# Moving the output projection's evacuation, root steps and row scaling off VectorE in a hybrid RG-LRU / stick-breaking-attention block

## The chip, the cores and the metric

The kernel runs as one program on one core of a Trainium2 chip. The metric is the device time of one execution in microseconds (us), as the median of several. The engines of the core are called here as the profile calls them: PE (TensorE, matrix products), DVE (VectorE), ACT (ScalarE), POOL (GpSimd) and SP (the queue from which all transfers of this kernel start). Each engine works through its own list of instructions in order. An instruction that waits for another engine holds up everything behind it on its own engine.

## The reference

One block of a language model on 2048 rows of width 1024, in float32:

```python
h  = rms_norm(x, norm_mix);  u = h @ w_in
lru_x, lru_g, q, k, v = split(u, [512] * 5)
y_lru = gelu(lru_g) * rg_lru(conv4(lru_x))            # linear recurrence over the rows
y_att = stick_breaking_attention(q, k, v)             # 8 heads of 64, causal
y  = concat(rms_norm(y_lru), rms_norm(y_att))
x  = x + y @ w_out                                    # the output projection
h2 = rms_norm(x, norm_ffn);  gu = h2 @ w_ffn_in
x  = x + (silu(gu[:2816]) * gu[2816:]) @ w_ffn_out
out = rms_norm(x, norm_final)
```

Stick-breaking attention has, for each query, `beta = sigmoid(z)` per key and a running product of `sigmoid(-z)` from the newest key to the oldest. The weight of a key is its beta times the product over the newer keys.

## The kernel before

Every float32 product is made of three products of split operands (`mm3`, L147 to L151: a high part rounded to fp32r, and a low part, the rest). The 2048 rows are four groups of 512 (`g`). The program has three stages: the mixer (up to some 1245 us), the first feed-forward product, and the second with the final norm. The change is in the mixer alone.

In the mixer the attention of group g is the main line (`attention`, `drive`), cut into items of 128 queries by up to 512 keys of one head. `drive` puts one iteration per item on the list and, between its steps, pieces of other work (the "fill"). Iteration i holds four steps of four different items:

- `score` of item i+4: PE forms `z`, ACT makes the two sigmoids `u` and `be` (L362, L363), POOL sets the last column of `u` to one (L360) and, in diagonal blocks, masks `u` and `be` (L366);
- `scan` of item i+2: the running product over `u` on DVE (L372);
- `weights` of item i+1: `be` times `u` on DVE (L378);
- `turn` of item i: PE transposes `be` into the PSUM tile `t`, ACT copies the high part `ah` out (L394), DVE takes the low part `al` (L395). Two iterations later `weigh` multiplies by the values (L408).

`u` has four buffers, `z` and `t` two each. For the first three groups the fill is the input projection of the next group. For the last group (from 805 us on) it is the output projection of all four groups, `mix_out`. It runs through eight jobs (g, br), br 0 for the recurrent half of y and br 1 for the attention half. A job (`Mix.run`) has eight PSUM tiles `po` of 128 rows by 512 columns, each the sum of 24 matmuls; after each, one DVE instruction (L671) multiplies the tile by the row's norm factor `rs` and adds it to the rows `x2` (named `xo` in the trace). After the second tile of a job `following.take` loads the four tiles `yt` of the next job, splits them (`yhi` on ACT, `ylo` on DVE L638), squares them on ACT and sums the squares on POOL (`acc`, L646). After the seventh tile `sums` has PE sum the squares over the channels (`pss`), and `rsqrt_mean` works out `rs` on tiles of 128x4: four DVE steps and three rounds of Newton's method with three DVE instructions each (L133, L135, L137).

After br 1 `store_rows` stores the rows and squares them on ACT (eight `sqf`, L695), and a second `rsqrt_mean` gives their factor `rsf` for the next norm. For the groups 0 and 1 `turn_rows` then scales the four row tiles, two on DVE (L707) and two on ACT (L705), waits `REST` = 8 pieces of fill during which only attention is on PE's list, and lets PE transpose the rows (`h2t`, L713). The last job, (3, 1), runs after the attention has ended.

PE's list is in the order in which the code is written (`manual_schedule`). The lists of DVE, ACT, POOL and SP are put in order by a scheduler that goes by its own estimates of durations and by priorities; the attention's steps have a higher priority than the fill. Small tiles of the fill (`yt`, `sqf`, the transposed rows `h`) share one pool, `stg` with tag `s`, of four buffers used in turn.

Of the kernel before, what the change touches and what calls it, by code (L numbers as in the profile page):

```python
# [9 lines left out]
F32 = mybir.dt.float32  # L10
F32R = mybir.dt.float32r
I32 = mybir.dt.int32
AF = mybir.ActivationFunctionType
ALU = mybir.AluOpType
# [3 lines left out]
P = 128  # L18
S = 2048
D = 1024  # L20
KD = D // P
LRU = 512
# [5 lines left out]
GT = 512  # L28
HT = 1024
NG = S // GT  # L30
TPG = GT // P
# [59 lines left out]
def tile_block(ctx: ExitStack, tc: tile.TileContext, x, w_in, w_out, w_gu, w_dn,  # L91
               g_mix, g_ffn, g_y, g_fin, lru_p, w_gate, out):
    nc = tc.nc
# [24 lines left out]

    smp = ctx.enter_context(tc.tile_pool(name="smp", bufs=2))

    def rsqrt_mean(ss, n, width, name):

        v = smp.tile([P, n], F32, tag=f"v{n}", name=f"{name}_v")
        nc.vector.tensor_scalar(out=v, in0=ss, scalar1=1.0 / width, scalar2=EPS, op0=ALU.mult, op1=ALU.add)  # L124
        t = smp.tile([P, n], I32, tag=f"t{n}", name=f"{name}_t")
        nc.vector.tensor_single_scalar(t, v.bitcast(I32), 1, op=ALU.arith_shift_right)
        y = smp.tile([P, n], F32, tag=f"y{n}", name=f"{name}_y", bufs=3)
        nc.vector.tensor_scalar(out=y.bitcast(I32), in0=t, scalar1=-1.0, scalar2=float(0x5F3759DF),
                                op0=ALU.mult, op1=ALU.add)
        nc.vector.tensor_scalar(out=v, in0=v, scalar1=-0.5, scalar2=None, op0=ALU.mult)  # L130
        for it in range(3):
            a = smp.tile([P, n], F32, tag=f"a{n}", name=f"{name}_a{it}")
            nc.vector.tensor_tensor(out=a, in0=y, in1=y, op=ALU.mult)  # L133
            b = smp.tile([P, n], F32, tag=f"b{n}", name=f"{name}_b{it}")
            nc.vector.tensor_tensor(out=b, in0=a, in1=v, op=ALU.mult)  # L135
            y2 = smp.tile([P, n], F32, tag=f"y{n}", name=f"{name}_y{it}", bufs=3)
            nc.vector.scalar_tensor_tensor(out=y2, in0=b, scalar=1.5, in1=y, op0=ALU.add, op1=ALU.mult)  # L137
            y = y2
        return y

# [2 lines left out]
    rsf = const.tile([P, S // P], F32, name="rsf")  # L143
# [14 lines left out]
    stg = base.enter_context(tc.tile_pool(name="stg", bufs=4, side="left"))  # L158
# [403 lines left out]
    def prep(g):  # L562
# [45 lines left out]
        for c in range(WC // P - 1):  # L608
            yield from proj_col(g, cg, c, w, keep_qk(g))
            if g == NG - 1:  # L610
                first[0].sums()

        turns = make_ht(g + 1, xs) if xs else iter(())
        for k, _ in enumerate(proj_col(g, cg, WC // P - 1, w, keep_qk(g))):
# [8 lines left out]
    class Mix:  # L623
# [21 lines left out]
                nc.scalar.activation(sq, yt, AF.Square)  # L645
                nc.gpsimd.tensor_tensor(out=self.acc, in0=self.acc, in1=sq, op=ALU.add)  # L646

        def sums(self):
            pss = ps_d.tile([P, GT], F32, tag="d", name=f"pss{self.nm}")
            for t in range(TPG):  # L650
                nc.tensor.matmul(pss[:, t:t + 1], lhsT=self.acc[:, t * P:(t + 1) * P], rhs=ones,
                                 start=True, stop=True)
            ss = smp.tile([P, TPG], F32, tag="ssy", name=f"ssm{self.nm}")
            nc.vector.tensor_copy(ss, pss[:, :TPG])
            self.rs = rsqrt_mean(ss, TPG, LRU, f"ry{self.nm}")

        def run(self, x2, following=None, ready=NCT):
            for n in range(D // GT):
                halves = [next_half(), next_half()]
                ns = slice(n * GT, (n + 1) * GT)  # L660
                for t in range(TPG):
                    ts = slice(t * P, (t + 1) * P)
                    po = ps_d.tile([P, GT], F32, tag="d", name=f"po{self.nm}_{n}_{t}")
                    for i, (hi, lo) in enumerate(halves):
                        for c in range(NCT):
                            yh, yl = self.split[c]
                            mm3(po[:, i * WC:(i + 1) * WC], yh[:, ts], yl[:, ts], hi[:, c], lo[:, c],
                                c == 0, c == NCT - 1)
                            if c == 1 or (c == NCT - 1 and i == 0):
                                yield  # L670
                    nc.vector.scalar_tensor_tensor(out=x2[t][:, ns], in0=po, scalar=self.rs[:, t:t + 1],  # L671
                                                   in1=x2[t][:, ns], op0=ALU.mult, op1=ALU.add)
                    yield
                    if following and (n, t) == (0, TPG // 2 - 1):
                        for c in range(ready):
                            following.take(c)
                    if following and ready == NCT and (n, t) == (1, SUMS):
                        following.sums()

    def load_rows(g):  # L680
        x2 = []
# [6 lines left out]
    def store_rows(g, x2):  # L688

        ss = smp.tile([P, TPG, 2], F32, tag="ssx", name=f"ssf{g}")  # L690
# [4 lines left out]
                nc.scalar.activation(sq, x2[t][:, i * 512:(i + 1) * 512], AF.Square, accum_out=ss[:, t, i:i + 1])  # L695
        s2 = smp.tile([P, TPG], F32, tag="ssy", name=f"ssg{g}")
        nc.vector.tensor_tensor(out=s2, in0=ss[:, :, 0], in1=ss[:, :, 1], op=ALU.add)
        nc.vector.tensor_copy(rsf[:, g * TPG:(g + 1) * TPG], rsqrt_mean(s2, TPG, D, f"rf{g}"))

    def turn_rows(g, x2):  # L700

        for t in range(TPG):
            r = rsf[:, g * TPG + t:g * TPG + t + 1]
            if t % 2:
                nc.scalar.activation(x2[t], x2[t], AF.Copy, scale=r)  # L705
            else:
                nc.vector.tensor_scalar(out=x2[t], in0=x2[t], scalar1=r, scalar2=None, op0=ALU.mult)  # L707
        for _ in range(REST):
            yield
        for k in range(KD):  # L710
# [558 lines left out]
```

## Time and profile before

| | |
|---|---|
| time, median of 3 runs | 2646.09 us (2645.66 to 2648.19) |
| profiled execution | 2647.3 us, its span 2645.6 us |
| PE busy, whole span | 2430.8 us (92%), mean granted clock 0.969 |
| DVE busy, whole span | 1842.4 us (70%) |
| ACT busy, whole span | 1262.6 us (48%) |
| POOL busy, whole span | 1204.0 us (46%) |

Busy shares are means over stages with different limits, so the rows of the section below are taken from the stage in question, 805 to 1195 us. A row that groups instructions gives line, engine, operation, tiles out and in, shapes and count, then busy time and mean duration of one, then the engine's idle time just before them and what ended it. In a timeline two instructions of one engine overlap a little: the next one starts some 0.08 us before the one ahead is recorded as ended.

### The profile page before, as it was taken

How to read it: one execution, taken by the hardware profiler on the slowest of the kernel's cores; microseconds unless marked ns; L12 is line 12 of the kernel's file. 1: busy time of each engine (PE TensorE's matmuls, PEld its weight loads, DVE VectorE, ACT ScalarE, POOL GpSimd, SP SyncE). 2: the span in 40 equal slices, each digit the busy share in tenths (PEclk: the TensorE clock that was granted, in tenths of full speed). 3: DMA queues.
4: the chain of work that ended last, by engine and by line, in shares of the span. 5: the costliest groups of instructions: out<-in, count | busy, mean ns of one | idle time of the engine just before them, and what ended most of it. 6: DMA issues, size and time to landing. Idle time of an engine off the chain costs nothing. (4 is left out here: it accounts for less than half of the span.)

```text
span 2645.6 us, 36918 instructions
## 1 busy us (share of the span) xinstructions
PE 2430.8 (92%) x12680; PEld 2046.7 (77%) x12680; DVE 1842.4 (70%) x2575; ACT 1262.6 (48%) x2285; POOL 1204.0 (46%) x1420
## 2 busy tenths in 40 slices
PE   7999999999888797897899979989999999999995
PEld 5888788787767697886777758868888887888884
DVE  4566888999999998997655545686655651644465
ACT  5556667576766575664333323343333322322233
POOL 5846433223244121122656654555545544744464
PEclk9999999999999898998999989999999999999997
DMA  7787886664556465654334443353232318745652
GB/s 249 266 288 250 269 267 211 209 210 143 176 179 208 152 223 169 206 188 151 123 121 137 157 167 100 108 177 114 100 103 97 111 69 323 257 153 183 196 172 104
DMA packets 221804, 468.57 MB, mean 177 GB/s; under 512 B 22704, under 2 KB 63664, under 8 KB 221616
## 3 DMA queue, kind: packets, MB, share of 16 engines
q1 hardware_dynamic: 221616, 466.21, 52.8%
q8 instruction: 100, 1.64, 0.3%
q14 instruction: 88, 0.72, 0.1%
HBM read 333.74 MB, written 132.38 MB: 176 GB/s over the span
## 5 line engine op out<-in xcount | busy, mean ns | idle before, releaser
L360 POOL MEMSET u<- 128x1 f32 x320 | 30.9, 98 | 559.2 <-DVE u L372 394.6
L372 DVE TENSOR_TENSOR_SCAN u<-u,u,zero 128x513 f32<-128x513 f32 x192 | 256.2, 1336 | 8.5 <-ACT u L362 8.0
L393 PE MATMUL t<-ident,be 128*128 128x128 f32 x1088 | 179.3, 281 | 59.0 <-DVE al L395 50.0
L378 DVE TENSOR_TENSOR be<-be,u 128x512 f32<-128x512 f32 (+2 forms) x320 | 215.4, 676 | 17.0 <-POOL be L366 1.4
L362 ACT ACTIVATE u<-z 128x512 f32<-128x512 f32 (+2 forms) x320 | 172.4, 539 | 99.1 <-PE z L358 65.2
L149 PE MATMUL pj<-ht_hi,w_hi 128*128 128x512 f32 x512 | 215.8, 421 | 2.3 <-DVE sl L291 1.5
L394 ACT CAST ah<-t 128x512 fp32r<-128x512 f32 (+2 forms) x320 | 168.7, 527 | 86.2 <-PE t L393 82.1
L393 PEld LDWEIGHTS t<-ident,be 128*128 128x128 f32 x1088 | 130.7, 143 | 98.5 <-DVE al L395 64.5
L151 PE MATMUL pj<-ht_hi,w_lo 128*128 128x512 f32 x512 | 202.8, 396 | 0.0
L150 PE MATMUL pj<-ht_lo,w_hi 128*128 128x512 f32 x512 | 201.9, 394 | 0.0
L358 PE MATMUL z<-ks,qd 128*128 128x512 f32 (+2 forms) x640 | 190.9, 380 | 7.1 <-ACT be L363 5.0
L395 DVE TENSOR_TENSOR al<-t,ah 128x512 fp32r<-128x512 f32 (+2 forms) x320 | 191.4, 599 | 7.5 <-ACT ah L394 7.1
L1088 POOL TENSOR_TENSOR e<-c,c 128x512 f32<-128x512 f32 x110 | 158.6, 1449 | 52.0 <-DVE c L1079 37.5
L363 ACT ACTIVATE be<-z 128x512 f32<-128x512 f32 (+2 forms) x320 | 172.5, 539 | 0.2
L408 PE MATMUL y<-ah,vs 128*128 128x256 f32 x576 | 149.9, 290 | 12.3 <-DVE yp L418 12.2
L149 PE MATMUL po<-wo_hi,yhi 128*128 128x256 f32 x512 | 154.9, 303 | 0.0
L372 DVE TENSOR_TENSOR_SCAN u<-u,zero 128x129 f32<-128x129 f32 (+3 forms) x128 | 112.3, 878 | 56.6 <-POOL u L366 55.0
L1141 DVE TENSOR_TENSOR blo<-dr,bhi 128x1024 fp32r<-128x1024 f32 (+1 forms) x41 | 81.8, 1995 | 98.5 <-ACT bhi L1140 98.5
L408 PE MATMUL y<-al,vs 128*128 128x256 f32 x576 | 147.8, 287 | 0.0
L151 PE MATMUL po<-wo_hi,ylo 128*128 128x256 f32 x512 | 145.7, 285 | 0.0
L150 PE MATMUL po<-wo_lo,yhi 128*128 128x256 f32 x512 | 145.6, 284 | 0.0
L1141 POOL TENSOR_TENSOR a0lo<-act,a0hi 128x1024 fp32r<-128x1024 f32 (+1 forms) x41 | 97.8, 2385 | 103.2 <-ACT a0hi L1140 103.2
(284 smaller groups left out, 7624.7 us busy)
## 6 DMA issues: line engine op xcount, KB each, us to landing
r<-in_w_gu SPq DMA_DIRECT2D x88, 512.0 KB, 3.9
act<-act_d SPq DMA_DIRECT2D x68, 512.0 KB, 4.2
dr<-in_w_dn SPq DMA_DIRECT2D x59, 512.0 KB, 4.5
act_d<-e SPq DMA_DIRECT2D x110, 256.0 KB, 2.0
w_hi<-w_d SPq DMA_DIRECT2D x50, 512.0 KB, 4.7
w_lo<-w_d SPq DMA_DIRECT2D x50, 512.0 KB, 5.5
vs<-vs_d SPq DMA_DIRECT2D x80, 256.0 KB, 3.6
ks<-ks_d SPq DMA_DIRECT2D x80, 256.0 KB, 3.6
```

Source lines behind the costliest of these rows:

```text
L149: nc.tensor.matmul(ps, lhsT=w_hi, rhs=m_hi, start=first, stop=False, skip_group_check=more)
L150: nc.tensor.matmul(ps, lhsT=w_hi, rhs=m_lo, start=False, stop=False, skip_group_check=more)
L151: nc.tensor.matmul(ps, lhsT=w_lo, rhs=m_hi, start=False, stop=last, skip_group_check=more)
L358: nc.tensor.matmul(z[:, :nz], lhsT=qd[:, i, qs], rhs=kss[p.c][:, :nz], start=i == 0, stop=i == 1)
L362: nc.scalar.activation(u[:, :n], z[:, :n], AF.Sigmoid, scale=-SCALE)
L363: nc.scalar.activation(be[:, :n], z[:, :n], AF.Sigmoid, scale=SCALE)
L372: nc.vector.tensor_tensor_scan(out=ur, data0=ur, data1=zero.broadcast_to([P, n + 1]), initial=1.0 if p.prev is None else p.prev.u[s][:, 0: ...
L378: nc.vector.tensor_tensor(out=p.be[s][:, :n], in0=p.be[s][:, :n], in1=p.u[s][:, 1:n + 1], op=ALU.mult)
L393: nc.tensor.transpose(tp[:, b, :], p.be[s][:, b * P:(b + 1) * P], ident)
L395: nc.vector.tensor_tensor(out=alo[:, :nb, s, :], in0=tp[:, :nb, :], in1=f32(ahi[:, :nb, s, :]), op=ALU.subtract)
L408: nc.tensor.matmul(y, lhsT=vs[:, b, :], rhs=t[:, b].rearrange("p s q -> p (s q)"), start=first and m == 0, stop=last and m == 1)
L1141: eng.tensor_tensor(out=lo, in0=src, in1=f32(hi), op=ALU.subtract)
```

## The change

Three edits, all in the mixer.

1. In every job of `Mix.run` but the last, the `po` tile leaves PSUM through ACT, which multiplies it by `rs` into a tile `pr` in SBUF, and POOL adds `pr` to the rows. `pr` is taken from the pool `stg`, tag `s`. That is 56 of the 64 tiles; the last job keeps the DVE instruction.
2. `rsqrt_mean` has its three Newton rounds on POOL for seven of the eight `rs` chains and for the `rsf` chains of the groups 0 to 2. POOL needs four instructions for a round, where DVE had three. The four steps ahead of the rounds stay on DVE.
3. `turn_rows` scales all four row tiles on ACT.

```diff
-    def rsqrt_mean(ss, n, width, name):
+    def rsqrt_mean(ss, n, width, name, pool=False):
...
         for it in range(3):
+            eng = nc.gpsimd if pool else nc.vector
...
-            nc.vector.tensor_tensor(out=a, in0=y, in1=y, op=ALU.mult)
+            eng.tensor_tensor(out=a, in0=y, in1=y, op=ALU.mult)
...
-            nc.vector.tensor_tensor(out=b, in0=a, in1=v, op=ALU.mult)
+            eng.tensor_tensor(out=b, in0=a, in1=v, op=ALU.mult)
...
-            nc.vector.scalar_tensor_tensor(out=y2, in0=b, scalar=1.5, in1=y, op0=ALU.add, op1=ALU.mult)
+            if pool:
+                eng.tensor_scalar(out=b, in0=b, scalar1=1.5, scalar2=None, op0=ALU.add)
+                eng.tensor_tensor(out=y2, in0=b, in1=y, op=ALU.mult)
+            else:
+                eng.scalar_tensor_tensor(out=y2, in0=b, scalar=1.5, in1=y, op0=ALU.add, op1=ALU.mult)
...
-                    nc.vector.scalar_tensor_tensor(out=x2[t][:, ns], in0=po, scalar=self.rs[:, t:t + 1],
-                                                   in1=x2[t][:, ns], op0=ALU.mult, op1=ALU.add)
+                    if following:
+                        pr = stg.tile([P, GT], F32, tag="s", name=f"pr{self.nm}_{n}_{t}")
+                        nc.scalar.activation(pr, po, AF.Copy, scale=self.rs[:, t:t + 1])
+                        nc.gpsimd.tensor_tensor(out=x2[t][:, ns], in0=pr, in1=x2[t][:, ns], op=ALU.add)
+                    else:
+                        nc.vector.scalar_tensor_tensor(out=x2[t][:, ns], in0=po, scalar=self.rs[:, t:t + 1],
+                                                       in1=x2[t][:, ns], op0=ALU.mult, op1=ALU.add)
...
-                        following.sums()
+                        following.sums(True)
...
-        nc.vector.tensor_copy(rsf[:, g * TPG:(g + 1) * TPG], rsqrt_mean(s2, TPG, D, f"rf{g}"))
+        nc.vector.tensor_copy(rsf[:, g * TPG:(g + 1) * TPG], rsqrt_mean(s2, TPG, D, f"rf{g}", g < NG - 1))
...
-            if t % 2:
-                nc.scalar.activation(x2[t], x2[t], AF.Copy, scale=r)
-            else:
-                nc.vector.tensor_scalar(out=x2[t], in0=x2[t], scalar1=r, scalar2=None, op0=ALU.mult)
+            nc.scalar.activation(x2[t], x2[t], AF.Copy, scale=r)
```

PE's list has the same products in the same order as before. Two places show what moves on the others.

On ACT, at the end of job (0, 1), before: `sqf0` are the squares of the rows of group 0, `u3`, `be3` and `ah3` are the attention of group 3, `yb3` is a copy for its result.

```order
L695 ACTIVATE sqf0_2_1_11512,ssf0_11498<-xo0_2_10097 128x512
L362 ACTIVATE u3_2_0_2_1_11421<-z3_2_0_2_1_11418 128x512
L363 ACTIVATE be3_2_0_2_1_11417<-z3_2_0_2_1_11418 128x512
L695 ACTIVATE sqf0_3_0_11515,ssf0_11498<-xo0_3_10099 128x512
L394 CAST ah3_2_0_3_11460<-t3_2_0_3_0_11464 128x128
L362 ACTIVATE u3_2_0_1_0_11480<-z3_2_0_1_0_11477 128x512
L363 ACTIVATE be3_2_0_1_0_11476<-z3_2_0_1_0_11477 128x512
L394 CAST ah3_2_0_3_11460<-t3_2_0_3_1_11491 128x2x128
L362 ACTIVATE u3_2_0_1_1_11555<-z3_2_0_1_1_11552 128x512
L363 ACTIVATE be3_2_0_1_1_11551<-z3_2_0_1_1_11552 128x512
L417 COPY yb3_1_1_0_11567<-y3_1_1_3_11244 64x256
L695 ACTIVATE sqf0_3_1_11517,ssf0_11498<-xo0_3_10099 128x512
```

The squares stand singly between steps of the attention. The same place on ACT now, from the last evacuation `pr` of the job on (the squares left out are four more of the same kind):

```order
L399 CAST ah3_2_0_3_11499<-t3_2_0_3_1_11532 128x2x128
L678 ACTIVATE pr0_1_1_3_11529<-po0_1_1_3_11449,ry0_1_y2_10742 128x512
L705 ACTIVATE sqf0_0_0_11541,ssf0_11539<-xo0_0_10096 128x512
L422 COPY yb3_1_1_0_11611<-y3_1_1_3_11276 64x256
L705 ACTIVATE sqf0_0_1_11543,ssf0_11539<-xo0_0_10096 128x512
L705 ACTIVATE sqf0_1_0_11546,ssf0_11539<-xo0_1_10098 128x512
...
L705 ACTIVATE sqf0_3_1_11558,ssf0_11539<-xo0_3_10102 128x512
L367 ACTIVATE u3_2_0_1_1_11599<-z3_2_0_1_1_11596 128x512
L367 ACTIVATE u3_2_0_0_0_11630<-z3_2_0_0_0_11627 128x512
L399 CAST ah3_2_0_2_11615<-t3_2_0_2_0_11617 128x4x128
```

All eight squares have come together behind the last evacuation, and the sigmoids of the next items stand behind them.

On POOL, in the first tiles of job (1, 0), before: `u3` and `be3` are the attention's tiles, `acc1_0` the sum of squares.

```order
L360 MEMSET u3_1_1_3_0_10944 128x1
L646 TENSOR_TENSOR acc1_0_10805<-acc1_0_10805,yt1_0_1_1_10987 128x512
L360 MEMSET u3_1_1_3_1_10972 128x1
L360 MEMSET u3_1_1_2_0_11053 128x1
L366 AFFINE_SELECT u3_1_1_3_0_10944<-u3_1_1_3_0_10944 128x128
L360 MEMSET u3_1_1_2_1_11077 128x1
```

The same place on POOL now, with the additions of `pr` to the rows `xo0`:

```order
L365 MEMSET u3_1_1_3_1_10998 128x1
L679 TENSOR_TENSOR xo0_0_10096<-pr0_1_0_0_10917,xo0_0_10096 128x512
L365 MEMSET u3_1_1_2_0_11079 128x1
L365 MEMSET u3_1_1_2_1_11105 128x1
L371 AFFINE_SELECT u3_1_1_3_0_10968<-u3_1_1_3_0_10968 128x128
L371 AFFINE_SELECT be3_1_1_3_0_10964<-be3_1_1_3_0_10964 128x128
L679 TENSOR_TENSOR xo0_1_10098<-pr0_1_0_1_10990,xo0_1_10098 128x512
L371 AFFINE_SELECT u3_1_1_3_1_10998<-u3_1_1_3_1_10998 128x128
```

Each addition stands between the attention's fills and masks and, in POOL's list, ahead of some of them.

## Rows read from the trace of the kernel before

**Rows 1.** Busy time by stretch (us, count): PE, PEld, DVE, ACT, POOL, PE's clock, DMA.

```profile
805.00:895.00 90.00, 78.49 (x595) 73.21 (x594) 88.42 (x121) 54.91 (x109) 35.50 (x72) 0.98 0.57 180
1045.00:1195.00 150.00, 136.08 (x1016) 127.14 (x1017) 139.71 (x230) 95.40 (x195) 27.56 (x87) 0.97 0.54 187
805.00:1195.00 390.00, 339.07 (x2516) 315.10 (x2515) 365.81 (x591) 245.20 (x501) 88.04 (x245) 0.95 0.57 189
```

**Rows 2.** PE's waits, 805 to 1195 us: total, times, longest.

```profile
PE t L393 <- DVE al L395: 27.1, 28, 2.4
PE h2t L713 <- DVE xo L707: 11.4, 2, 6.5
```

**Rows 3.** DVE's groups, 805 to 1195 us.

```profile
L372 DVE TENSOR_TENSOR_SCAN u<-u,u,zero 128x513 f32<-128x513 f32 x90 | 119.0, 1323 | 3.0 <-ACT u L362 2.7
L378 DVE TENSOR_TENSOR be<-be,u 128x512 f32<-128x512 f32 x98 | 72.3, 739 | 3.7
L395 DVE TENSOR_TENSOR al<-t,ah 128x512 fp32r<-128x512 f32 x98 | 66.5, 679 | 4.3 <-ACT ah L394 4.2
L671 DVE SCALAR_TENSOR_TENSOR xo<-po,ry_y,xo 128x512 f32<-128x512 f32 x53 | 39.1, 737 | 0.0
L638 DVE SCALAR_TENSOR_TENSOR ylo<-yt,gy,yhi 128x512 fp32r<-128x512 f32 x27 | 22.3, 830 | 1.0 <-ACT yhi L637 1.0
L135 DVE TENSOR_TENSOR ry_b<-ry_a,ry_v 128x4 f32<-128x4 f32 x18 | 3.3, 186 | 0.4
L707 DVE TENSOR_SCALAR xo<-xo,rsf 128x1024 f32<-128x1024 f32 x4 | 2.8, 750 | 0.1
```

**Rows 4.** POOL's groups, 805 to 1195 us.

```profile
L646 POOL TENSOR_TENSOR acc<-acc,yt 128x512 f32<-128x512 f32 x20 | 32.1, 1604 | 13.9 <-ACT yt L645 12.9 <-PE po L151 0.7
L229 POOL TENSOR_TENSOR wo_lo<-wo_raw,wo_hi 128x256 fp32r<-128x256 f32 x16 | 16.5, 1057 | 0.2 <-ACT wo_hi L226 0.2
```

**Rows 5.** Timeline of DVE and POOL, 814 to 825 us: start, duration.

```profile
814.20 0.74 DVE L638 SCALAR_TENSOR_TENSOR ylo<-yt,gy,yhi 128x512 fp32r<-128x512 f32 x1
815.69 1.94 POOL L646 TENSOR_TENSOR acc<-acc,yt 128x512 f32<-128x512 f32 x1 [2.32 <-ACT yt L645]
816.47 1.72 DVE L638 SCALAR_TENSOR_TENSOR ylo<-yt,gy,yhi 128x512 fp32r<-128x512 f32 x1
...
818.99 3.29 POOL L646 TENSOR_TENSOR acc<-acc,yt 128x512 f32<-128x512 f32 x2 [1.36 <-ACT yt L645]
819.37 1.78 DVE L378 TENSOR_TENSOR be<-be,u 128x512 f32<-128x512 f32 x1
821.07 0.68 DVE L395 TENSOR_TENSOR al<-t,ah 128x512 fp32r<-128x512 f32 x1
821.67 1.70 DVE L372 TENSOR_TENSOR_SCAN u<-u,u,zero 128x513 f32<-128x513 f32 x1
...
823.94 0.67 DVE L378 TENSOR_TENSOR be<-be,u 128x512 f32<-128x512 f32 x1
824.54 1.27 DVE L372 TENSOR_TENSOR_SCAN u<-u,u,zero 128x513 f32<-128x513 f32 x1
```

**Rows 6.** ACT's groups, 805 to 1195 us.

```profile
L695 ACT ACTIVATE sqf<-xo 128x512 f32<-128x512 f32 x24 | 15.1, 631 | 26.4 <-DVE xo L671 24.9 <-DVE ry_a L133 1.4
L715 ACT ACTIVATE h<-h2t,gf 128x512 f32<-128x512 f32 x16 | 11.3, 727 | 4.0 <-PE h2t L713 4.0
L705 ACT ACTIVATE xo<-xo,rsf 128x1024 f32<-128x1024 f32 x4 | 4.4, 1141 | 8.4 <-DVE rsf L698 8.4
```

**Rows 7.** Timeline from the last product of job (0, 1) to the transposes of its rows.

```profile
902.89 0.28 PE L151 MATMUL po<-wo_hi,ylo 128*128 128x256 f32 x1
...
906.37 0.75 DVE L671 SCALAR_TENSOR_TENSOR xo<-po,ry_y,xo 128x512 f32<-128x512 f32 x1
...
912.91 0.16 DVE L697 TENSOR_TENSOR ssg<-ssf 128x4 f32<-128x4 f32 x1
...
920.78 1.42 DVE L707 TENSOR_SCALAR xo<-xo,rsf 128x1024 f32<-128x1024 f32 x2
...
921.59 1.14 PE L713 MATMUL h2t<-ident,xo 128*128 128x128 f32 x3 [6.53 <-DVE xo L707]
923.02 0.47 PE L713 MATMUL h2t<-ident,xo 128*128 128x128 f32 x1 [0.29 <-ACT xo L705]
```

More of the change, by code (lines that the diff above doesn't have):

```diff
@@ L610, in prep @@
             if g == NG - 1:
-                first[0].sums()
+                first[0].sums(True)
         turns = make_ht(g + 1, xs) if xs else iter(())
@@ L646, in take, with sums @@
                 nc.gpsimd.tensor_tensor(out=self.acc, in0=self.acc, in1=sq, op=ALU.add)
-        def sums(self):
+        def sums(self, pool=False):
             pss = ps_d.tile([P, GT], F32, tag="d", name=f"pss{self.nm}")
@@ L654, in sums @@
             nc.vector.tensor_copy(ss, pss[:, :TPG])
-            self.rs = rsqrt_mean(ss, TPG, LRU, f"ry{self.nm}")
+            self.rs = rsqrt_mean(ss, TPG, LRU, f"ry{self.nm}", pool)
         def run(self, x2, following=None, ready=NCT):
```

## The prediction

> **What bounds the kernel now.** I read the busy time by stretch first, then PE's waits in the stretch that the change touches, then the groups of instructions of DVE, POOL and ACT there, and last two timelines.
>
> The change acts where the output projection is the fill of the attention, from 805 to about 1195 us. Over the whole span PE is the fullest engine, but in these 390 us it is DVE: 365.8 us busy against PE's 339.1, ACT's 245.2 and POOL's 88.0 [rows 1]. In the first 90 us DVE is at 98% and PE idles 11.5 us; in the last 150 us DVE is at 93% and PE idles 13.9 us. PE's waits say the same: 28 times it waits for the low part `al` of the transposed weights, 27.1 us in all, and twice, 11.4 us in all, for the scaled rows before it may transpose them [rows 2]. DVE's own idle time ahead of its large groups is a few us [rows 3], so in these stretches it sets the pace. Work taken off DVE can shorten the stage, until PE is full.
>
> **What the change takes from DVE.** 56 evacuations (53 of them recorded before 1195 us) at 0.737 us [rows 3]; the records of successive DVE instructions overlap by 0.08 us, so each holds DVE for 0.66 us: 56 x 0.66 = 37 us. The Newton rounds of the `rs` chains: three groups of 18 instructions like L135's [rows 3], 3.3 us each, 9.8 us in all, less 54 x 0.08: 5.5 us. The two scaled row tiles per group, 2.8 us [rows 3], and the rounds of the `rsf` chains lie in the wait for the transposes and are counted there. Sum: 42.5 us off DVE.
>
> **What comes back.** Each evacuation becomes an addition on POOL of two SBUF tiles of 128x512. The nearest row is `acc`, the same operation, shapes and place: 1.604 us [rows 4], so 56 x 1.6 = 90 us more on POOL. It has the room (88 of 390 us used). But the timeline shows that DVE pays for such an addition. While `acc` runs from 815.69 to 817.63, `ylo` takes 1.72 us, where 0.74 is what it takes alone; under the next two, `be` takes 1.78 (alone 0.67) and the scan 1.70 (alone 1.27), while `al`, which reads PSUM, keeps its 0.68 [rows 5]. The instruction that goes, L671, reads PSUM as `al` does; the one that comes is of the kind that slows DVE.
>
> The price has two ends. The three cases of rows 5 add 0.98 + 1.11 + 0.43 = 2.5 us of DVE to 5.23 us of POOL: 0.48 us per us. Over the whole stretch the means stand above what these instructions take alone by 0.07 us for 98 `be`, 0.05 for 90 scans and 0.09 for 27 `ylo` [rows 3, 5]: 6.9 + 4.5 + 2.4 = 13.8 us, over 32.1 + 16.5 = 48.6 us of POOL arithmetic [rows 4]: 0.28 us per us. I take 0.3, near the mean, because it covers meetings with `al` and with idle gaps too: 90 x 0.3 = 27 us come back (ends 25 and 43). DVE's net relief is 42.5 - 27 = 15.5 us (ends -0.5 and 17.5).
>
> The Trainium skill, page "SBUF — State Buffer", section "Who interferes with whom", says that a DVE instruction with two inputs in SBUF and a GpSimd instruction that reads SBUF exclude each other: whichever comes second waits for the whole of the first, while one with a single SBUF input is not touched. By that rule `ylo`, begun at 816.47 under an addition that ends at 817.63, would end at 817.63 + 0.74 = 818.37; the trace has 818.19, so it agrees.
>
> **What reaches the end.** A us off DVE shortens the stage only where PE waits for DVE. PE's idle time in the two stretches of rows 1 is 25 us of 240; elsewhere PE is full or waits for the rows. I let half of the relief through: -8 us.
>
> **The other edits and the waits they add.** On ACT 56 evacuations come in at 0.73 us (L715, the nearest: PSUM to SBUF with a factor per partition [rows 6]), 41 us, and two more row scalings per group at 1.14 us, 4.6 us. ACT goes from 245 to 291 of 390 us. It waits there for DVE's evacuation before it can square rows, 24.9 us [rows 6], and that wait goes; but an evacuation that waits for PE now holds up the sigmoids and casts behind it. DVE's work, which goes on beside ACT's, hides the one and the other, and I cost the two at nothing together; if that cover fails, it is 41 less 24.9, 16 us.
>
> POOL's additions wait for ACT. Behind them stand the fills and masks of `u`, which the scan needs two iterations later, some 6 us; an addition of 1.6 us fits, and I cost it at nothing (at the other end 1 us for each of the 30 or so diagonal items that PE notices: some 5 us). The tiles `pr` share the four `s` buffers with `yt`: the last two loads of `yt` now wait on SP for POOL's additions, but are needed five tiles of PE later. The stores of the rows wait for POOL instead of DVE; nothing before the next stage reads them.
>
> **The row chain, twice.** Before, the last product of job (0, 1) starts at 902.89, DVE takes it up only at 906.37, the sum of squares follows at 912.91, the scaling at 920.78, and PE transposes from 921.59, the fourth tile at 923.02: 20.1 us [rows 7]. After: evacuation 0.7, the block of eight squares 8 x 0.63 = 5.0 with the last addition under it, sum 0.2 (6 us, where 10 were); two small steps, 0.4; two scans and four other instructions of the attention that DVE's list holds ahead of the rest, 5.2; one more scan, for whose buffer POOL waits inside the chain, 1.3; twelve POOL steps; a copy, 0.2; four scalings on ACT, 4 x 1.1 = 4.4 where two engines shared them in 2.2. POOL's steps on 128x4 are in no row. DVE's like steps take 0.19 us [rows 3], POOL's smallest sum in the rows, on 128x256, 1.06 [rows 4]: 12 steps are between 2.3 and 12.7 us, and by size 3 is the likelier. Sum 20.5 us, so +0.5 for each of two groups (at worst +10 each). The attention's sigmoids wait behind the squares, but PE, which has only attention on its list there, stops at the transposes in either kernel. Together +1.
>
> **Sum.** -8 + 1 = -7 us. The profiled execution took 2647.3 us, 1.2 above the median of 2646.1; from the former that is 2640, from the median 2639, which I give.
>
> **Rivals.**
>
> *PE becomes the bound.* If additions meet mostly `al` and gaps, or ACT's freed waits bring sigmoids and casts forward, DVE stops being last and PE's 25 idle us in the stretches of rows 1 shrink to some 3: -22, 2624. For it: 27.1 us of PE's waits are for one DVE instruction. Against: rows 5.
>
> *Nothing arrives.* At the dearer price, 43 us, DVE's relief is gone, and waits and row chain cancel what is left: 2646, within 3.
>
> *Slower: POOL's additions cost DVE more than they save.* The case decides at 42.5 / 56 = 0.76 us of DVE per addition. The single addition of rows 5 cost `ylo` 0.98; DVE is busy nearly all the time, and most of its time is scans and products with two SBUF inputs. At 0.98 an addition 56 cost 55 us, DVE has 12.5 us more than before, and three quarters of it shows, since DVE already sets the pace: +9, 2655. Against it: the mean of the whole stretch, 0.28 x 1.6 = 0.45 us per addition. Under the same rule of the page "SBUF — State Buffer" of the Trainium skill this is the case in which every addition meets such an instruction at its start.
>
> **How the numbers follow.** The forecast has 0.42, its own range 2632 to 2644; PE as the bound 0.20; nothing arrives 0.18; slower 0.20. A measurement here tells about 0.2%, 5.3 us, from no change. Of the forecast about four fifths is beyond that (0.34), with PE's case 0.54 faster; 0.08 + 0.18 the same, 0.26; 0.20 slower. The range 2621 to 2653 leaves out the far ends of PE's case and of the slower one.
>
> **What would show it.** In the trace after: DVE's busy share between 805 and the end of the attention falls only to 92 or 93%, with `be` near 0.85 us, scans near 1.38 and `al` unchanged; PE's wait for `al` falls to about 15 to 20 us; POOL's additions take 1.5 to 1.7 us; the transposes of group 0 begin 19 to 21 us after the last product. Scans near 1.6 us and `be` above 1.0 would mean the slower case; PE at 96% in the first 90 us its opposite; POOL steps of 0.5 us or more would make the row chain the loss. The two stages behind the mixer should take as long as before.

## The result and the profile after

The changed kernel takes 2674.9 us (median of 4 runs, 2672.6 to 2676.5) against 2645.9 before: ratio 1.0107, with a 95% interval of 1.0090 to 1.0125. It is slower by 29 us, where 2639 was forecast, and lies outside the range. In the trace after, the lines from `rsqrt_mean` on stand 1 to 10 lower (L671 is now L678 and L679, L372 is L377, L395 is L400).

Busy time by stretch, in the columns of [rows 1]:

```profile
805.00:895.00 90.00, 75.73 (x555) 70.29 (x554) 79.53 (x94) 59.46 (x112) 61.09 (x93) 0.96 0.52 173
1045.00:1195.00 150.00, 120.44 (x861) 110.62 (x860) 123.10 (x166) 101.63 (x208) 65.05 (x148) 0.92 0.54 185
805.00:1195.00 390.00, 322.40 (x2351) 297.66 (x2350) 328.11 (x428) 264.33 (x523) 192.08 (x381) 0.94 0.54 181
```

DVE has room: 328 us busy in place of 366. But PE did not use it. It is busy 17 us less, with fewer instructions in the same time, so part of DVE's fall is work that has not come yet. No engine is full any more: the stage is paced by waits, and PE's waits name them (compare [rows 2]):

```profile
PE t L398 <- DVE al L400: 30.5, 29, 3.4
PE z L363 <- ACT be L368: 22.8, 8, 8.8
PE h2t L720 <- ACT xo L714: 12.6, 8, 4.7
```

The wait for `al` has not fallen, and one for ACT's sigmoids, under 2 us before, has come. DVE's groups, to hold against [rows 3], and below them its own waits, of which the first was 8.8 us before and the second was not there:

```profile
L377 DVE TENSOR_TENSOR_SCAN u<-u,u,zero 128x513 f32<-128x513 f32 x85 | 127.7, 1505 | 6.7 <-POOL u L365 3.4 <-ACT u L367 3.0
L383 DVE TENSOR_TENSOR be<-be,u 128x512 f32<-128x512 f32 x91 | 73.4, 808 | 7.5 <-ACT ah L399 0.9 <-ACT u L367 0.5
L400 DVE TENSOR_TENSOR al<-t,ah 128x512 fp32r<-128x512 f32 x91 | 61.9, 680 | 2.3 <-ACT ah L399 2.2
```

```profile
DVE u L377 <- POOL u L371: 21.2, 10, 4.9
DVE ssg L707 <- ACT sqf L705: 16.0, 3, 5.8
```

The scan rose from 1.323 to 1.505 us and `be` from 0.739 to 0.808, while `al`, which reads PSUM, stayed. On POOL, beside [rows 4], the additions and one of the root steps on 128x4:

```profile
L679 POOL TENSOR_TENSOR xo<-pr,xo 128x512 f32<-128x512 f32 x48 | 72.7, 1514 | 3.8 <-ACT be L368 2.3 <-ACT pr L678 1.5
L651 POOL TENSOR_TENSOR acc<-acc,yt 128x512 f32<-128x512 f32 x18 | 27.8, 1543 | 14.4 <-ACT yt L650 14.0
L139 POOL TENSOR_SCALAR ry_b<-ry_b 128x4 f32<-128x4 f32 x18 | 8.7, 481 | 1.4
```

From PE's first product of the output projection to its last, the same PE instructions stand in every kernel, so that stretch can be compared whole. The columns are those above; the lines are the kernel before, the kernel after, and two runs of the section below, e14 and e12:

```profile
800.70:1241.60 440.90, 382.39 (x2842) 356.89 (x2841) 408.18 (x658) 268.96 (x547) 104.06 (x260) 0.95 0.55 183
805.20:1273.30 468.10, 388.94 (x2843) 361.56 (x2841) 392.55 (x517) 308.51 (x607) 223.51 (x424) 0.93 0.51 173
802.70:1213.80 411.10, 375.82 (x2843) 353.94 (x2841) 372.42 (x594) 297.92 (x596) 101.53 (x259) 0.96 0.56 187
801.20:1255.40 454.20, 390.17 (x2843) 362.42 (x2841) 407.93 (x595) 298.82 (x597) 190.22 (x315) 0.93 0.52 175
```

For the same work DVE is busy 15.6 us less after than before, and the stretch is 27.2 us longer. PE stands idle 20.7 us more in it, and is busy 6.6 us more, at a lower mean granted clock. The stretch starts 4.5 us later, and behind it the program takes 1404 us before and 1401 after, so the loss is in the mixer.

The row chain of group 0, which [rows 7] show for the kernel before (start, duration, and in brackets the wait ahead of it):

```profile
911.76 0.28 PE L156 MATMUL po<-wo_hi,ylo 128*128 128x256 f32 x1
...
912.64 0.71 ACT L678 ACTIVATE pr<-po,ry_y 128x512 f32<-128x512 f32 x1
...
912.80 1.27 DVE L377 TENSOR_TENSOR_SCAN u<-u,u,zero 128x513 f32<-128x513 f32 x1
...
912.88 1.19 POOL L140 TENSOR_TENSOR ry_y<-ry_b,ry_y 128x4 f32<-128x4 f32 x1
...
914.88 0.61 ACT L705 ACTIVATE sqf<-xo 128x512 f32<-128x512 f32 x1
...
916.59 0.20 POOL L140 TENSOR_TENSOR ry_y<-ry_b,ry_y 128x4 f32<-128x4 f32 x1
...
916.77 1.26 POOL L679 TENSOR_TENSOR xo<-pr,xo 128x512 f32<-128x512 f32 x1
...
918.06 0.63 ACT L705 ACTIVATE sqf<-xo 128x512 f32<-128x512 f32 x1 [2.47 <-POOL xo L679]
...
921.26 1.09 ACT L367 ACTIVATE u<-z 128x512 f32<-128x512 f32 x2
...
921.26 0.16 DVE L707 TENSOR_TENSOR ssg<-ssf 128x4 f32<-128x4 f32 x1 [5.83 <-ACT sqf L705]
...
923.17 1.13 ACT L368 ACTIVATE be<-z 128x512 f32<-128x512 f32 x2
...
923.86 1.22 PE L363 MATMUL z<-ks,qd 128*128 128x512 f32 x2 [8.77 <-ACT be L368]
...
924.56 0.20 POOL L134 TENSOR_TENSOR rf_a<-rf_y 128x4 f32<-128x4 f32 x1
...
926.86 1.28 DVE L377 TENSOR_TENSOR_SCAN u<-u,u,zero 128x513 f32<-128x513 f32 x1
...
927.10 1.04 POOL L136 TENSOR_TENSOR rf_b<-rf_a,rf_v 128x4 f32<-128x4 f32 x1 [0.61 <-DVE rf_v L130]
...
931.10 0.20 POOL L140 TENSOR_TENSOR rf_y<-rf_b,rf_y 128x4 f32<-128x4 f32 x1
...
931.34 0.26 DVE L708 COPY rsf<-rf_y 128x4 f32<-128x4 f32 x1 [2.39 <-POOL u L365]
...
931.63 4.27 ACT L714 ACTIVATE xo<-xo,rsf 128x1024 f32<-128x1024 f32 x4 [2.72 <-DVE rsf L708]
...
935.95 0.48 PE L720 MATMUL h2t<-ident,xo 128*128 128x128 f32 x1 [0.56 <-ACT xo L714]
```

Read it from the fourth square, at 918.06. It waits for the last addition's `s` buffer: the ring has four, and the square takes the one of the last `pr`. That addition, whose `pr` was done at 913.35, starts only at 916.77, because the root steps of the next job stand ahead of it on POOL. Four sigmoids and two casts stand behind the squares on ACT, so PE, which has not reached the transposes yet, stops for 8.77 us at `z`.

### The profile page after: what moved, and what is told of

Its sections match the earlier page's. It is cut to its first block, busy times and chain, and to the rows that moved or that the text cites. A ratio compares the mean times of both kernels' runs of the same rounds, so it can differ in the third digit from the quotient of the medians.

```text
span 2674.4 us, 37049 instructions
## 1 busy us (share of the span) xinstructions
PE 2437.0 (91%) x12680; PEld 2050.6 (77%) x12680; DVE 1824.7 (68%) x2425; ACT 1302.6 (49%) x2345; POOL 1324.8 (50%) x1596
## 5 line engine op out<-in xcount | busy, mean ns | idle before, releaser
L377 DVE TENSOR_TENSOR_SCAN u<-u,u,zero 128x513 f32<-128x513 f32 x192 | 271.4, 1415 | 12.6 <-ACT u L367 8.7
L383 DVE TENSOR_TENSOR be<-be,u 128x512 f32<-128x512 f32 (+2 forms) x320 | 227.7, 714 | 23.6 <-POOL be L371 2.9
L400 DVE TENSOR_TENSOR al<-t,ah 128x512 fp32r<-128x512 f32 (+2 forms) x320 | 191.0, 598 | 5.7 <-ACT ah L399 5.3
L377 DVE TENSOR_TENSOR_SCAN u<-u,zero 128x129 f32<-128x129 f32 (+3 forms) x128 | 113.7, 889 | 73.4 <-POOL u L371 71.8
```

The costliest lines, as they stand in the source:

```text
L377: nc.vector.tensor_tensor_scan(out=ur, data0=ur, data1=zero.broadcast_to([P, n + 1]), initial=1.0 if p.prev is None else p.prev.u[s][:, 0: ...
L383: nc.vector.tensor_tensor(out=p.be[s][:, :n], in0=p.be[s][:, :n], in1=p.u[s][:, 1:n + 1], op=ALU.mult)
L400: nc.vector.tensor_tensor(out=alo[:, :nb, s, :], in0=tp[:, :nb, :], in1=f32(ahi[:, :nb, s, :]), op=ALU.subtract)
```

## Experiments

All are built from the kernel before or from the changed kernel by one edit or a few. Ratios are to runs of the kernel before on the same chip, whose median was 2645.7 to 2646.6 us. A ratio is not the quotient of the two medians; the two differ by up to 0.001, some 2.6 us, so differences of that size between runs are not sure. e13 and e14 leave part of the sum out of the rows.

| run | what it is | median us | ratio, 95% interval |
|---|---|---|---|
| e1_evac | evacuation alone | 2667.3 | 1.0071 (1.0053 to 1.0089) |
| e12_evac_own | the same, `pr` in own buffers | 2661.0 | 1.0055 (1.0038 to 1.0072) |
| e2_roots | root steps alone | 2645.0 | 0.9992 (0.9982 to 1.0001) |
| e3_scale | row scaling alone | 2652.1 | 1.0017 (1.0006 to 1.0028) |
| e4_own | all three, `pr` in own buffers | 2667.7 | 1.0075 (1.0060 to 1.0090) |
| e10_last2 | as e4, last two tiles of a group on DVE | 2665.1 | 1.0064 (1.0049 to 1.0080) |
| e13_noevac | no evacuation, no addition | 2621.4 | 0.9898 (0.9883 to 0.9913) |
| e14_noadd | ACT's part alone, nobody adds | 2622.2 | 0.9902 (0.9887 to 0.9917) |
| e5_dveadd | ACT scales, DVE adds | 2651.1 | 1.0014 (1.0003 to 1.0026) |
| e8_actcopy | idle ACT copies beside DVE's work | 2650.3 | 1.0010 (1.0000 to 1.0020) |
| e6_dummy | idle POOL additions beside DVE's work | 2673.2 | 1.0093 (1.0075 to 1.0112) |
| e9_fills | POOL fills as long as additions | 2653.7 | 1.0027 (1.0018 to 1.0037) |
| e7_dummyms | the same fills, all between 735 and 864 us | 2666.0 | 1.0065 (1.0045 to 1.0084) |
| e11_ry | root steps inside the jobs only | 2641.0 | 0.9980 (0.9970 to 0.9991) |
| e15_accdma | 32 of the 56 additions by transfers | 2636.0 | 0.9954 (0.9940 to 0.9967) |
| e16_accall | 50 of 56 by transfers | 2637.9 | 0.9963 (0.9949 to 0.9976) |
| e17_both | e15 and e11 | 2635.3 | 0.9957 (0.9942 to 0.9972) |
| e18_rows | e17, one transfer for a row tile | 2633.1 | 0.9948 (0.9932 to 0.9965) |

e2, e3 and e5 came out some 1 us outside the range of their theory; larger misses are named below.

**The three edits apart, and the ring.** The edits are those of the diff, one at a time. In e4_own and e12_evac_own `pr` has two buffers of its own, in a pool that is idle by then:

```diff
-  pr = stg.tile([P, GT], F32, tag="s", name=f"pr{self.nm}_{n}_{t}")
+  pr = lrp.tile([P, GT], F32, tag="xc", name=f"pr{self.nm}_{n}_{t}", bufs=2)
```

> Only the evacuation is changed (ACT scales the projection's sums out of PSUM, GpSimd adds them to the rows); the root steps and the row scaling stay as before. Theory (the loss comes from work that now stands in a row on ACT and GpSimd: the squares of a finished group wait for the last addition on GpSimd, the diagonal masks wait behind additions): most of the 29 us is here, 2662 to 2668, and the squares start about 2 us sooner than in the full change, since no root steps stand ahead of the last addition. Rival contention (the additions stretch the vector engine's scans, and only that counts): 2665 to 2675, with the scans as long as in the full change (1.50 us against 1.32). Rival roots (the root steps on GpSimd are the loss): 2646 or less.

> Only the root steps are changed (Newton rounds of the mixer on GpSimd). Theory: about twelve steps of 0.4 us in place of nine of 0.07 to 0.15 us in a chain that PE waits for three times, against 5.5 us off a vector engine that bounds the stage: 2646 to 2651. Rival roots: 2660 or more, with the transposes of each finished group some 4 us later than before.

> Only the row scaling is changed (all four tiles of a finished group on ACT). Theory: four scalings of 1.1 us in a row in place of two beside two, twice, so 2 x 2.3 us later transposes, of which the vector engine's relief gives some back: 2646 to 2651. Rival (nothing of it reaches the end, since PE has other work): 2645 to 2647.

> The full change with the scaled sums in buffers of their own instead of the four that the tiles of the mixed heads and the squares share. Theory: the fourth square of a group no longer waits for a buffer, but still for the last addition, which comes from the same queue: 3 x 1 to 2 us sooner, 2669 to 2674. Rival (the shared ring alone makes the squares late): 2658 to 2664. Rival contention: no change, 2673 to 2677.

> Evacuation alone as in the change (ACT scales, GpSimd adds; roots and row scaling as before), but the scaled sums in buffers of their own. Theory (the shared ring holds up the fourth square of a group, and PE waits at z behind ACT's squares): 5 to 8 us less than the same with the shared ring, 2659 to 2662. Rival (the ring only mattered together with the root steps on GpSimd): 2665 to 2668.

Evacuation alone carries 21 of the 29 us. The shared ring costs 6 us of it by the medians (e1 less e12; 4 by the ratios, whose intervals overlap) and 7 in the whole change (after less e4; 8 by the ratios). e4 lies between the ranges of its theory and of its ring rival. PE's wait for the sigmoids shows it, first evacuation alone with the ring, then with own buffers:

```profile
PE z L358 <- ACT be L363: 13.9, 8, 5.1
```

```profile
PE z L358 <- ACT be L363: 2.3, 3, 1.6
```

So the ring, and not the last addition alone, made the squares late, and it does so without POOL's root steps too. With own buffers the squares still wait 19 us for POOL's additions, but PE's wait at `z` is nearly gone. In the full change, own buffers take the same wait from 22.8 to 6.0 us, but only 7 of these 17 us reach the end. The scaling costs about 5 us (4.5 by its ratio, 6 by the medians). PE's wait for the scaled rows is 15.7 us (12.0 before), and a block of four scalings on ACT makes the sigmoids, and so the masks, late:

```profile
DVE u L372 <- POOL u L366: 15.7, 8, 6.8
```

The root steps alone can't be told from no change. But one part of them can be seen in the traces: the root of the first job stands on POOL ahead of a mask, for which DVE waits 3.7 us at 796, and PE behind it waits for `al` 2 us longer than before. In the four kernels that have this root on POOL (after, e2, e4, e10) PE starts the projection at 803.4 to 805.7 us, 804.6 in the mean; in the other kernels but e7 it starts at 800.3 to 804.7, 802.0 in the mean.

**What the relief is worth, and ACT's part.** Both runs leave the sums of the first seven jobs out of the rows.

```diff
-  nc.vector.scalar_tensor_tensor(out=x2[t][:, ns], in0=po, ...)     # both; the last job keeps it
+  pr = lrp.tile([P, GT], F32, tag="xc", ...)                        # e14_noadd only
+  nc.scalar.activation(pr, po, AF.Copy, scale=self.rs[:, t:t + 1])  # e14_noadd only
```

> The kernel before without the 56 scalings with additions of the first seven jobs at all, on no engine: their part of the sum is left out of the rows. This prices what 41 us off the vector engine are worth when nothing comes back. My prediction took half of a relief to reach the end: 2646 - 20 = 2626. Rival (the order on PE and the chain through transposes, sigmoids, scan and split set the pace, whatever the vector engine's share): 2636 to 2644. Rival (the vector engine is the bound at 94%): 2605 to 2615.

> ACT scales the sums of the first seven jobs out of PSUM into buffers of their own, and nobody adds them to the rows: their part of the sum is left out. Against the run without any evacuation it prices ACT's 56 x 0.73 us; against the run with evacuation in own buffers it prices GpSimd's additions. Theory: ACT costs about 4 us (as the idle copies did) over the run without evacuation, 2630 to 2642, and the additions the 20 to 25 us from there to 2660. Rival ACT: 2650 or more.

56 instructions of 0.737 us less on DVE are worth 25 us: 0.6 us per us taken off. The runs free more than DVE's time, though: the squares of the rows wait for no evacuation any more (24.9 us of ACT's waits before [rows 6]), and the two row chains are 3.4 and 4.3 us shorter in e14 than before. How much of the 25 us that is was not separated. ACT's 56 scalings on top cost 1 us, which can't be told from nothing. e13 lies between its theory and the rival of DVE as the bound, e14 under its range. The way from e14 to e12 is the price of POOL's additions with all that waits for them: 39 us, 0.69 each. The traces of e14, then of e12, 805 to 1195 us, DVE's scans and `be`, PE's wait for `al` and DVE's for the masks:

```profile
L372 DVE TENSOR_TENSOR_SCAN u<-u,u,zero 128x513 f32<-128x513 f32 x93 | 122.9, 1322 | 3.7 <-ACT u L362 3.5
L378 DVE TENSOR_TENSOR be<-be,u 128x512 f32<-128x512 f32 x102 | 76.3, 748 | 7.1
PE t L393 <- DVE al L395: 17.5, 16, 3.7
DVE u L372 <- POOL u L366: 7.7, 7, 3.3
```

```profile
L372 DVE TENSOR_TENSOR_SCAN u<-u,u,zero 128x513 f32<-128x513 f32 x86 | 125.9, 1464 | 3.6 <-ACT u L362 3.3 <-POOL xo L674 0.2
L378 DVE TENSOR_TENSOR be<-be,u 128x512 f32<-128x512 f32 x95 | 79.6, 838 | 7.1 <-ACT ah L394 0.5
PE t L393 <- DVE al L395: 32.8, 32, 2.6
DVE u L372 <- POOL u L366: 15.1, 14, 3.2
```

Without the additions PE's wait for `al` does fall, to the 15 to 20 us of the prediction; the additions bring it back, and double the wait for the masks.

**Reads or queue.** Beside DVE's unchanged work stands an addition whose result nobody reads (e6), ACT's copy alike (e8), or three fills of 0.53 us (e9, e7). In e5 ACT scales and DVE adds:

```diff
+  nc.gpsimd.tensor_tensor(out=dm, in0=x2[t][:, ns], in1=x2[t][:, ns], op=ALU.add)   # e6
+  nc.scalar.activation(dm, po, AF.Copy, scale=self.rs[:, t:t + 1])                  # e8
+  nc.gpsimd.tensor_copy(dm[:, 0:1], x2[t][:, n * GT:n * GT + 1])                    # e9
+  for _ in range(3): nc.gpsimd.memset(dm, 0.0)                                      # e9, e7
```

> The kernel before, with the sums scaled out of PSUM by ACT into a buffer of their own and added to the rows by the vector engine, so that GpSimd adds nothing. The vector engine keeps some 0.5 to 0.6 us for each in place of 0.66, ACT does 56 x 0.73 us more. Theory (GpSimd's additions are the loss, by their queue and by what they do to the scans): 2644 to 2650. Rival ACT (the 41 us more on ACT, in line with sigmoids and copies that PE waits for, are the loss): 2655 to 2665.

> The kernel before, whose vector engine still does all 56 scalings with additions, and beside each of them an addition on GpSimd whose result nobody reads. Rival contention: the scans stretch as in the full change (26 us over the stage) on a vector engine that has nothing taken off: 2668 to 2680. Queue theory (what hurts is that masks and sums of squares stand behind an addition that comes late): the scans stretch, but the additions wait for nothing but the rows: 2652 to 2665.

> The kernel before, and behind each of the 56 scalings with additions three fills of a 128x512 tile on GpSimd, which read nothing and stand in its queue. Rival contention: fills do not touch the scans' reads, so 2645 to 2650 with scans at 1.32 us. Queue theory: the masks come later by up to the length of the fills, as the vector engine's waits for masks show (8.8 us before, 21 in the full change): 2650 to 2660.

> The kernel before, whose vector engine still does all 56 scalings with additions, and beside each a scaled copy of the same sums out of PSUM on ACT whose result nobody reads. Rival ACT: 2655 to 2665 (41 us more on ACT, at 63% before). Theory (ACT's copies alone are cheap): 2646 to 2651.

> The kernel before, and behind each of the 56 evacuations three GpSimd fills of a 128x512 tile (0.52 us each, 1.6 us together, as long as an addition), held in place by a copy of one column of the row just written. They read nothing but that column. The earlier run with fills had them all between 735 and 863 us; here they are spread as the additions are. If reading is what costs (contention): 2646 to 2650, against 2673 with the idle additions. If the queue alone costs (masks and sums of squares behind 1.6 us of other work): 2655 to 2665.

The idle additions cost 27 us, as much as contention by itself was to cost, though the scans stretched to 1.377 us alone and not to the 1.50 that the rival named; `be` took the larger part, 0.850. The fills, which read nothing and hold POOL for longer (56 x 2.1 us with the copy of a column), cost 7.5 us, between the two ranges of their expectation, and leave the scans alone. DVE's scans, `be` and wait for the masks with the additions, then with the fills:

```profile
L372 DVE TENSOR_TENSOR_SCAN u<-u,u,zero 128x513 f32<-128x513 f32 x86 | 118.4, 1377 | 2.8 <-ACT u L362 2.7
L378 DVE TENSOR_TENSOR be<-be,u 128x512 f32<-128x512 f32 x93 | 78.9, 850 | 4.8 <-POOL be L366 1.1
DVE u L372 <- POOL u L366: 9.0, 11, 3.2
```

```profile
L372 DVE TENSOR_TENSOR_SCAN u<-u,u,zero 128x513 f32<-128x513 f32 x88 | 115.8, 1316 | 3.0 <-ACT u L362 2.7
L378 DVE TENSOR_TENSOR be<-be,u 128x512 f32<-128x512 f32 x97 | 73.1, 755 | 4.1 <-POOL be L366 0.2
DVE u L372 <- POOL u L366: 15.0, 16, 3.2
```

So some 20 of the 27 us go with the reads, if the place in POOL's queue costs an addition what it costs the fills, 7. That last part is not shown: under the fills DVE waits 15.0 us for the masks, under the idle additions 9.0, as before (8.8). e7 was meant as e9, but the scheduler put all 168 fills between 735 and 864 us, far ahead of most evacuations; packed like that the fills alone cost 20 us, more than either of its ranges, and PE starts the projection at 809 us. ACT's copies, and DVE's addition in two steps, cost 4 and 5 us, little against 39.

**The additions elsewhere.** In e15 ACT writes the first branch's scaled sums into the rows' tile, and the input's rows are added by an accumulating transfer; e16 does the second branch alike through a buffer, but for the last two tiles of a group.

```diff
-  nc.sync.dma_start(out=xt, in_=x[g * GT + t * P:g * GT + (t + 1) * P, :])
...
+  if following and not self.br:
+      nc.scalar.activation(x2[t][:, ns], po, AF.Copy, scale=self.rs[:, t:t + 1])
+      nc.gpsimd.dma_start(out=x2[t][:, ns], in_=x[self.g * GT + t * P:self.g * GT + (t + 1) * P, ns],
+                          accum_op=ALU.add)
```

e10 is e4 with `not (self.br and n and t >= TPG - 2)` added to the condition of the new branch; e11 passes `pool=True` in `following.sums` alone.

> The kernel before, with a third place for the addition: in the first branch's jobs ACT writes the scaled sums straight into the rows' tile, and the input's rows are added to it by a transfer that accumulates, issued from GpSimd; the second branch's jobs stay on the vector engine. 28 evacuations leave the vector engine, and no engine adds. Theory (the additions cost by GpSimd's reads and its queue, 39 us for 55, while a relief of 41 us is worth 25 and ACT's part about 1): 28 issues of GpSimd cost little, so half the relief, 2646 - 12 = 2634 to 2640. Rival (an addition anywhere but on the vector engine comes late and holds the chain): 2650 or more.

> As the run with the accumulating transfer, and in the second branch's jobs too ACT scales into a buffer that a transfer adds to the rows; only the last two tiles of a group stay on the vector engine, so that the squares wait for no transfer. 50 of 56 evacuations leave the vector engine. Theory: 2646 - 50 x 0.45 = 2624 to 2634. Rival: 2655 or more; transfers that land late would show as waits of ACT's squares and of the vector engine for rows.

> The kernel before, with the Newton rounds on GpSimd only for the root of the mixed heads inside the mixer's jobs (not for the first job's root, not for the finished rows' root, which stay on the vector engine). Theory (those three rounds are on no path, the row root is): all of the relief of 6 x 9 x 0.16 = 9 us less the extra of GpSimd, worth 0.6 us per us, no row chain lengthened: 2640 to 2645. Rival (nothing to be seen, as with all root steps moved): 2644 to 2647.

> The full change with own buffers for the scaled sums, and the last two tiles of each finished group evacuated by the vector engine as before (6 of 56), so that the squares of the group do not wait for GpSimd. If the wait of the squares for the last addition is what stays (ACT waits 28 us in all for GpSimd at the squares with own buffers): 2655 to 2661 against 2668. Rival (spread over all 50 other additions, 0.7 us each): 6 x 0.7 less, 2663 to 2666.

e15 gains 10.6 us with 32 evacuations off DVE (four jobs of eight, not the 28 that its expectation counts): here the additions could leave DVE, where no engine read for them. e16 takes 18 more from DVE and gains nothing by them, a miss: 50 issues of 0.87 us stand in POOL's queue, and DVE waits 19.9 us for the masks, where e15 has 9.1. ACT's squares wait 19.8 us for the late transfers, but in e15 they wait as long for DVE (22.4). That the masks are the reason is argued and was not tested by itself. The issues are those of the whole run, the wait is that of 805 to 1195 us:

```profile
L677 POOL DMA_DIRECT2D xo<-in_x x32 | 28.0, 876 | 22.0 <-ACT xo L676 10.3 <-DMA wo_lo<-wo_d 5.2 <-issue 2.1
DVE u L372 <- POOL u L366: 19.9, 13, 4.3
```

e10 gains 2.6 us over e4, no more than the 4 that 6 of 56 additions cost at the general price: nothing shows the last ones to be special once the ring is not shared. e11 gains 5.5 us where all root steps together gain 1, so the rounds of the finished rows and of the first job's root, which e2 moves as well, seem to cost some 4 to 5; the intervals of e11 and e2 overlap. The later start of the projection is some 2.5 of it.

> The two edits that were faster by themselves, together: the first branch's sums scaled by ACT with the input's rows added by accumulating transfers, and the Newton rounds of the mixed heads' root on GpSimd inside the mixer's jobs. If the two gains add (10.6 and 5.5 us): 2629 to 2633. If the second is eaten by GpSimd's queue, in which 32 issues of 0.88 us now stand as well: 2634 to 2638.

> The same two edits, with one accumulating transfer for a whole row tile of 1024 columns in place of two of 512, so 16 issues on GpSimd in place of 32. If an issue costs as much for the larger transfer (0.88 us) and its queue is what masks wait in: 2 to 4 us less than with two. If the issue grows with the size, or the transfers were hidden: no difference (within 2 us).

The two gains do not add: e17 is within a us of e15. One transfer in place of two takes 2 us more off, within what the runs scatter; its issue is hardly longer than that of half the size (0.906 against 0.876 us), and halving the issues took 13 us off POOL:

```profile
L679 POOL DMA_DIRECT2D xo<-in_x x16 | 14.5, 906 | 18.7 <-ACT xo L677 16.0 <-issue 1.1 <-ACT be L368 0.7
```

The fastest kernel that does all the work is e18_rows, 12.7 us under the kernel before.

## Why the prediction was wrong

The parts, priced one on another by medians: 2646 - 25 (DVE's evacuations gone) + 1 (ACT) + 39 (POOL's additions) + 6 (the ring) + 8 (roots and scaling on top) = 2675. Each part is good to a few us.

- **DVE's sum was right.** Predicted were 42.5 us off and 27 back, 15.5 net, and DVE is busy 15.6 us less over the same PE work. Counted instruction by instruction, as the time above what the same form takes when it meets no POOL arithmetic, DVE lost some 20 us to POOL before and some 46 after, 23 to 29 more by where the stage is cut.
- **"I let half of the relief through" is the step that failed.** It netted 42.5 against 27 and took half of the rest, as if a us of DVE were worth the same on both sides, so that less DVE time had to mean less time. The relief by itself was worth 25 us, 0.6 per us taken off. The additions cost not 27 x 0.5 = 13.5 us, but 39. By DVE's busy time over the same PE work, e13 has 31 us less for its 25 us (0.8 per us), e12 has 36 more than e14 for 39 (1.1), and e6 has 21 more than before for 27 (1.3). Why the two differ is argued: what went was an evacuation, for which the third PSUM tile after it waits, and the squares at a group's end; what came is in scans and `be`, in the chain for which PE's transposes wait, and in POOL's queue ahead of the masks.
- **How the 39 divide** is shown in part. Idle additions cost 27; the other 12 come with additions that wait for ACT and are waited for. In the two executions that the result section shows whole, e12's stretch is 43 us longer than e14's: 29 us are PE's idle time (its wait for `al` is 18 us longer, for `y` 5), and 14 us are PE being busy longer with the same instructions, at a mean granted clock of 0.93 against 0.96. So a third of the price is paid at a lower clock. After its stop of 8.77 us in group 0 of the changed kernel PE has a granted clock of 0.50 from 924 to 928 us, the lower of its two levels (1.2 GHz), and a product of `y` takes 0.41 us, where it took 0.28 ahead of the stop. Whether the waits account for all of the lower clock wasn't settled.
- **"I cost the two at nothing together"** was right for ACT's load: +1 us in e14, +4 with the idle copies of e8.
- **Masks "at the other end ... some 5 us"**: DVE's wait for the masks rose from 8.8 to 21.2 us. What that is worth at the end is not shown for additions; fills of 2.1 us each cost 7.5 us.
- **"The tiles `pr` share the four `s` buffers ...: the last two loads of `yt` now wait"** looked at the wrong sharer. It was the fourth square that waited, and it held the sigmoids: 6 to 7 us where nothing was put.
- **"PE ... stops at the transposes in either kernel"** was wrong: PE stopped before them, at `z`, for 8.8 us in group 0.
- **The row chain** was put at 20.5 us and took 24.2 (911.76 to 935.95; 20.1 before). In group 1 it took 25.5, where 21.5 were before. So the two chains are 8 us longer, where "together +1" was put; in e1, whose roots and scalings stay as before, they take 20.5 and 23.0. The root of the first job, which the prediction leaves out, adds some 2.5. The squares were not done 5.7 us after the last product's evacuation began, but 8.5; the POOL steps took 6.7 us (924.56 to 931.30) instead of 3, since one DVE step stands between them in DVE's list behind the attention, and a scan then holds POOL up; the four scalings took 4.3, as said.
- **"Slower" as a rival** had its sign and its engine right, but its point of decision, 0.76 us of DVE per addition, was never reached: it was 26/56 = 0.46. The change was slower with DVE relieved, for which no rival stood.
- **What would show it:** `be` at 0.81 (0.85 said), additions at 1.51 (1.5 to 1.7), `al` unchanged, the transposes 21.1 us after the last product (19 to 21) and the stages behind the mixer (1401 against 1404 us) came out; scans at 1.505 were above 1.38, DVE's share of 84% far below the 92 to 93%, and the wait for `al` of 30.5 far above 15 to 20. A share that falls more than the work removed says that the engine waits.

## What to carry to other kernels

Price what leaves an engine and what comes to it apart, each by where it stands: here the work that went was worth less per us than the stretch that came, and a sum of one engine's busy time had the wrong sign. Before moving additions to GpSimd beside VectorE work on two SBUF operands, run the move with the additions left out and with idle additions; here the two runs gave the gain (25 us) and two thirds of the price (27 of 39). A tile put into a shared ring belongs to everyone's wait list: count which later user lands on its buffer, and what stands behind that user on its engine.

## What the runs showed of the hardware

- The stretch goes both ways. At 912.88 a POOL product on 128x4, 0.20 us alone (916.59), takes 1.19 us and ends at 914.07 with the scan that began at 912.80, in the kernel after. By the Trainium skill, page "SBUF — State Buffer", section "Who interferes with whom", an instruction of DVE with two SBUF inputs and a GpSimd instruction that reads SBUF keep each other out, while one that only writes does not meet it. The traces agree in both parts: the product ended with the scan, and under the 168 fills of e9 the scans took 1.316 us, where they took 1.323 before.
- A copy of one column (128x1) on POOL took 0.553 us in the mean of 56 (e9).
- An accumulating transfer into SBUF was issued by POOL in 0.876 us for 256 KB (e16) and 0.906 us for 512 KB (e18), and landed 5.7 and 7.0 us after (medians).
- The changed kernel's PE had a lower granted clock in the last stretch of [rows 1], 0.92 against 0.97 (means over its two levels, 1.2 and 2.4 GHz), while it was busy less: 120 us of 150 against 136.
